# Branch projections of a hybrid encoder: loads handed out further ahead, four operand slots in an idle tile

## Chip, cores and metric

One NeuronCore of one Trainium2 chip runs the whole kernel. The metric is device time in microseconds (us) of one launch, the median of several runs. Everything is float32 at the interface.

## The reference, cut to what matters

One encoder layer over 1024 tokens (and 16 learned ones) of width 1024: a combined input projection, a gated DeltaNet branch A, a short-convolution branch B, a gated merge of the two, an output projection, and a SwiGLU. The change touches the place where the two branches are projected, merged and projected again:

```python
o = o * lax.rsqrt(jnp.mean(o * o, axis=-1, keepdims=True) + RMS_EPS) * norm_w
o = o * jax.nn.silu(z)                               # 8 heads of 128: (L, 1024)
y_a = o_dn @ w_branch_dn[l]
y_b = (sc_b * depthwise_conv_centred(sc_c * sc_x, sc_conv_w[l])) @ w_branch_sc[l]
merged = jax.nn.sigmoid(gate_a) * y_a + jax.nn.sigmoid(gate_b) * y_b
h_res = h_res + merged @ w_out[l]
```

## The kernel before, in words

**Splitting.** A float32 matrix product is done as three fast products: each operand is split into a high part (a cast on ScalarE, ACT: `hi`, here the ring `parts_h`) and a low part (VectorE, DVE, subtracts: `al`), and TensorE (PE) adds hi x hi, lo x hi and hi x lo (lines 1854 to 1856 in `products`, in varying order of the operands).

**Strassen-like quads.** Each of the two 1024 x 1024 x 1024 branch projections is done in seven products of half-size blocks (`QUADS`; S and T are sums of blocks, most of them prepared in DRAM). Each product of a quad has four 128-row tiles k of depth; two of them, a *k-pair*, make one **turn** q of the loop at the end of the stage. So a branch has 14 turns: 0 to 13 are branch B (z = 0), 14 to 27 are branch A (z = 1). A turn is 24 matmuls of 128 x 512. Turn pairs alternate between two groups of four PSUM banks, but turns 12, 13 and then 14, 15 use the same group.

**One turn.** `parts(q + 2)` casts and subtracts the operands of the turn after next (two tiles of 128 x 1024 each, so an `al` pair on DVE); `load(q + 4)` issues the DMAs of a later turn; `products(q)` is PE's work; `taken(q)`, after odd turns, copies or adds the four banks into running sums (`pv`, `us`) and, after four of the seven quads, multiplies them by gate tiles into `mA` and `mB`; `beside` lists the other work of the turn. The order of SPq (SyncE's DMA queue, on which all these DMAs are issued), DVE and ACT is the order in which this code is written (`manual_schedule`); only PE's order is chosen by a scheduler. In both kernels it puts the first four matmuls of turn 16 in front of turn 14, and six hi x hi and hi x lo products in front of the first product that needs `wl` in the output projection behind the stage (lines 1942 to 1944).

**Buffers.** `load` takes `rawtile` slots: four, in rotation. Branch B takes two of 512 KB per turn (four DMAs of 256 KB), branch A one. A slot is free when the `al` subtraction that reads it is done. `s4` tiles (four, in rotation) hold gate tiles and the z of a head. The large tiles `b0` to `b3` hold the first turns' operands (`b0`, `b1`), branch A's operand `og` (`b2`: heads 0 to 3, `b3`: heads 4 to 7), block sums of it (`b1`), and in the end the split `w_out` (`woh`, `wol`).

**Beside the turns.** `gated(h)` prepares head h of branch A: for h below 4 it only loads z (already multiplied); for h of 4 to 7 it loads o and z and multiplies them on DVE (line 1755) in the same place. `gate_tiles` loads four gate tiles; `block_sums` forms the sums of `og` (line 179); `out_load` and `out_split` load and split `w_out`, one of eight row tiles each; `merged(0)` splits the first rows of the merged result (`wh`, `wl`).

Of the kernel before, what the change touches and what calls it, by code (L numbers as in the profile page):

```python
# [8 lines left out]
F32 = mybir.dt.float32  # L9
# [3 lines left out]
ALU = mybir.AluOpType  # L13
# [3 lines left out]
P = 128  # L17
D = 1024
KT = 8
SEQ = 1024  # L20
# [8 lines left out]
ZH = 4  # L29
# [19 lines left out]
def encoder_layer(ctx: ExitStack, tc: tile.TileContext, x, meta, norm1_w, w_in, w_ba,  # L49
                  dn_conv_w, A_log, dt_bias, dn_norm_w, sc_conv_w, w_bdn, w_bsc,  # L50
                  w_out, norm2_w, w_gu, w_down, final_w, out):
    nc = tc.nc
    x, out = x[0], out[0]
# [11 lines left out]
    def uid(s):  # L65
        cnt["n"] += 1
        return f"{s}_{cnt['n']}"

    def s4(n=1024):
        return tp.tile([P, 1024], F32, tag="s4", name=uid("s4"), bufs=4)[:, :n]  # L70
# [29 lines left out]
    def split(hi, lo, src):  # L100
        nc.scalar.copy(hi, src)  # L101
        nc.vector.tensor_tensor(out=lo, in0=src, in1=hi.bitcast(F32), op=ALU.subtract)  # L102
# [3 lines left out]
    def rawtile(shape):  # L106
        raw_slots.append(raw_slots.pop(0))
        pool, tag = raw_slots[-1]
        return pool.tile(shape, F32, tag=tag, name=uid("raw"), bufs=1)
# [111 lines left out]
    z_d = [dr.tile([P, SEQ], F32, name=f"z_d{i}") for i in range(H)]  # L221
    o_d = [dr.tile([P, SEQ], F32, name=f"o_d{i}") for i in range(KT)]
# [4 lines left out]
    cols = keep.tile([P, 25], F32, name="cols")  # L227
# [854 lines left out]
    with tc.tile_pool(name="st", bufs=1) as st:  # L1082
# [7 lines left out]
        raw = st.tile([P, KT, 32], F32, name="wba_raw")  # L1090
# [371 lines left out]
    def big(tag, shape, dtype=F32R):  # L1462
        return tp.tile(shape, dtype, tag=tag, name=uid(tag))
# [239 lines left out]
        steps[k]()  # L1703
    border0.close()
    QUADS = (("A11", "B11"), ("A12", "B21"), ("S2", "T2"), ("S1", "T1"), ("S3", "T3"), ("S4", "B22"), ("A22", "T4"))
    loads = {}

    def load(q):

        z, n, kk = q // 14, q % 14 // 2, q % 2  # L1710
        a, b = QUADS[n]
        w, w_sums = ((w_bsc, ss_d), (w_bdn, sd_d))[z]
        plain = {"A11": (0, lo), "A12": (4, lo), "A22": (4, hi), "B11": (0, hi), "B21": (4, hi), "B22": (4, lo)}
        summed = {"S2": (0, lo), "S3": (0, hi), "S4": (1, lo), "S1": (1, hi), "T3": (0, lo), "T1": (0, hi), "T2": (1, lo), "T4": (1, hi)}
        loads[q] = []
        for x in (a, b)[:2 - z]:
            raw = rawtile([P, 2, 512])
            loads[q].append(raw)
            for i in range(2):
                k = 2 * kk + i  # L1720
                if x in plain:
                    r, c = plain[x]
                    src = w[(r + k) * P:(r + k + 1) * P, c] if x[0] == "A" else p_d[r + k][:, c]
                else:
                    r, c = summed[x]
                    src = (w_sums if x[0] == "S" else ts_d)[k][:, r, c]
                nc.sync.dma_start(raw[:, i], src)
# [11 lines left out]
        for i in range(2):  # L1739
            nc.sync.dma_start(ts_d[k][:, i], r[i])  # L1740

    og = []

    def gated(h):

        if not og:
            og.extend(big(f"b{2 + i}", [P, 4, SEQ], F32) for i in range(2))
        ot = og[h // 4][:, h % 4]
        if h < ZH:
            nc.sync.dma_start(ot, z_d[h])  # L1750
            return
        nc.sync.dma_start(ot, o_d[h])
        sz = s4(SEQ)
        nc.sync.dma_start(sz, z_d[h])
        nc.vector.scalar_tensor_tensor(out=ot, in0=ot, scalar=cols[:, 24:25], in1=sz, op0=ALU.mult, op1=ALU.mult)

    for n, j in enumerate(range(GH + 2, KT - 1), 2):
        d = pair_steps(n, j)[0]
        for i, k in enumerate(PAIR.split()):
            d[k]()  # L1760
            if i in (4, 16):
                state_sums(2 * n - 4 + i // 16)
    load(0)
    o1 = last_pair(KT - 1 - GH, KT - 1)

# [58 lines left out]
    woh, wol, raw_out = [], [], []  # L1824

    def out_load(j):
        raw_out.append(rawtile([P, D]))
        nc.sync.dma_start(raw_out[j], w_out[j * P:j * P + P, :])

    def out_split(j):  # L1830
        if j % 4 == 0:
            for w, tags in ((woh, ("b0", "b1")), (wol, ("b2", "b3"))):
                t = big(tags[j // 4], [P, 4, D])
                w.extend(t[:, k] for k in range(4))
        split(woh[j], wol[j], raw_out[j])
# [3 lines left out]
    def parts(q):  # L1839

        z, n, kk = q // 14, q % 14 // 2, q % 2
        operands[q] = *part(loads[q][0]), *part(loads[q][1] if z == 0 else o_blocks[QUADS[n][1]][:, 2 * kk:2 * kk + 2])

    def products(q):

        z, n, kk = q // 14, q % 14 // 2, q % 2
        bank = (bank_x, bank_y)[n % 2]
        fresh = n in (0, 1, 3)
        ah, al, bh, bl = operands[q]
        for t in range(4):  # L1850
            c = slice(t * P, t * P + P)
            for k in range(2):
                begin, end = kk + k == 0, kk + k == 2
                mm(bank[t], ah[:, k, c], bh[:, k], start=begin and fresh, stop=False, skip_group_check=not fresh)
                mm(bank[t], ah[:, k, c], bl[:, k], start=False, stop=False, skip_group_check=not fresh)
                mm(bank[t], al[:, k, c], bh[:, k], start=False, stop=end, skip_group_check=not fresh)

    def taken(q):

        z, n, kk = q // 14, q % 14 // 2, q % 2  # L1860
        bank = (bank_x, bank_y)[n % 2]
        if not kk:
            return
        if not pv:
            w = big("w2", [P, 2, 512], F32)
            pv.extend([w[:, 0], w[:, 1], *(tp.tile([P, 512], F32, tag="t2", name=uid("t2"), bufs=2) for _ in range(2))])
        if n == 2 and not us:
            w = [wp.tile([P, 2, 512], F32, tag=g, name=uid("us"), bufs=2) for g in ("wh", "wl")]
            us.extend(w[t // 2][:, t % 2] for t in range(4))
        for t, y in enumerate(bank):  # L1870
            if n in (0, 3):
                nc.scalar.copy(pv[t], y)
            elif n == 2:
                nc.scalar.copy(us[t], y)
            elif n in (1, 4):
                add(pv[t], y, pv[t])
            elif n == 5:
                add(us[t], y, us[t])
        if n not in where:
            return  # L1880
        r, c = where[n]
        for t in range(4):
            y, g, m_ = (us if n == 5 else bank if n == 6 else pv)[t], gates[z, n][t], mg[r // 4][:, t, c]
            nc.vector.scalar_tensor_tensor(out=g if z else m_, in0=g, scalar=1.0, in1=y, op0=ALU.add, op1=ALU.mult)
        if z:
            for t in range(4):
                m_ = mg[r // 4][:, t, c]
                add(m_, m_, gates[z, n][t])

    def merged(t):  # L1890
        mh, ml = wtiles([P, KT, P])
        for i in range(2):
            split(mh[:, 4 * i:4 * i + 4], ml[:, 4 * i:4 * i + 4], mg[i][:, :, t * P:(t + 1) * P])
        xr = s4(D)
        nc.sync.dma_start(xr, x[t * P:(t + 1) * P])
        return mh, ml, xr

    beside = {0: [(gated, 4)], 1: [(gate_tiles, 0, 1)], 2: [(gated, 5)], 3: [(gated, 6)], 4: [(gated, 0)], 5: [(gated, 7)],
              6: [(gate_tiles, 0, 4), (gated, 1)], 7: [(gated, 2)], 8: [(gated, 3), (gate_tiles, 0, 5)],
              9: [(block_sums, 0)], 10: [(block_sums, 1)], 11: [(gate_tiles, 0, 6)], 12: [(block_sums, 2)],  # L1900
              15: [(gate_tiles, 1, 1)], 16: [(block_sums, 3)], 18: [(out_load, 0)], 19: [(out_load, 1)],
              20: [(gate_tiles, 1, 4), (out_split, 0), (out_load, 2)], 21: [(out_split, 1), (out_load, 3)],
              22: [(gate_tiles, 1, 5), (out_split, 2), (out_load, 4)], 23: [(out_split, 3), (out_load, 5)],
              24: [(gate_tiles, 1, 6), (out_load, 6)], 25: [(out_split, 4), (out_split, 5), (out_load, 7)],
              26: [(out_split, 6), (out_split, 7)]}
    load(1)
    parts(0)
    parts(1)
# [4 lines left out]
    for q in range(28):  # L1913
        if q + 2 < 28:
            parts(q + 2)
        if q + 4 < 28:
            load(q + 4)
        products(q)
        if q == 27:
            first_rows = merged(0)  # L1920
        taken(q)
        for f, *a in beside.get(q, ()):
            f(*a)
# [56 lines left out]
    def part1(w, p1, sg):  # L1980

        rg, ru, A_ = w
        bank = pss()
        product(bank, A_["A11"], "B11")
        nc.scalar.copy(p1, bank)
        po = psz()
        product(po, A_["A12"], "B21")
        add(sg, po, p1)
        nc.scalar.activation(sg, sg, AF.Silu)
        return rg, ru, A_, p1, sg, bank  # L1990
# [191 lines left out]
    for j in range(2, NF):  # L2182
# [6 lines left out]
        else:  # L2189
            rg, ru, A_, p1, sg, b1 = part1(stationary1(j), sm[:, (j + 1) % 2], sm[:, 2 + (j + 1) % 2])  # L2190
# [4 lines left out]
        if j >= HK:  # L2195
            k = j - HK
# [166 lines left out]
```

## Time and profile before

| | us |
|---|---|
| median of 3 runs | 1981.32 (1979.26 to 1981.97) |
| the profiled execution, its own time | 1978.7 |
| its span, first to last instruction | 1977.0 |
| the changed stage, first to last matmul start | 1062.35 to 1240.81 |
| PE clock granted, mean of the span | 0.994 |

In the profile a line names an engine, a line of the code, an operation, what is written and read, and its shape; in a timeline the first two numbers are start and duration in us, and a bracket gives the idle time of that engine before the row and what ended it. SPq rows are DMA issues, not transfers. Rows of a line that stand together are merged (x2).

### The profile page before, as it was taken

Reading aid. Unit: us, or ns where it says so; the run is one execution under the profiler, and the core shown is the slowest. Engines: PE = TensorE matmul, PEld = TensorE weight load, DVE = VectorE, ACT = ScalarE, POOL = GpSimd, SP = SyncE. Lnnn points to the kernel's source line nnn. Section 1 sums busy time; section 2 is a strip of 40 time slices with the busy share of each in tenths; the row PEclk is TensorE's granted clock in tenths of the full one; section 3 lists DMA queues with packets and bytes.
Section 4 is the critical chain, followed back from the end, with each engine's and each line's share of the span. In section 5 each row is a group of like instructions: output and inputs, shape, how many; then the busy total and the mean of one; then the engine's idle time right before and its main releaser. Section 6 shows DMA issues by size and latency. Waiting matters only on the chain. (4 is left out here: it accounts for less than half of the span.)

```text
span 1977.0 us, 32151 instructions
## 1 busy us (share of the span) xinstructions
PE 1942.7 (98%) x11896; PEld 1706.0 (86%) x11896; DVE 1477.2 (75%) x3121; ACT 875.2 (44%) x2016; POOL 109.2 (6%) x410
## 2 busy tenths in 40 slices
PE   9999999999999999999999789999999999999998
PEld 8999999999999999888888668788888888888887
DVE  7888688888888888868963488669676766746575
ACT  6462364646464645343434345235332333324344
POOL 2011101010101010100000000000000000000000
PEclk9999999999999999999999899999999999999999
DMA  4122122212121223376367656223366654487654
GB/s 145 63 84 81 56 85 60 83 52 85 51 87 50 86 59 98 108 264 241 111 246 252 225 203 208 96 86 116 119 224 249 243 185 163 170 277 244 192 177 164
DMA packets 141987, 286.15 MB, mean 145 GB/s; under 512 B 46909, under 2 KB 48374, under 8 KB 138374
## 3 DMA queue, kind: packets, MB, share of 16 engines
q1 hardware_dynamic: 141237, 283.05, 42.7%
q8 instruction: 93, 1.52, 0.3%
q10 hardware_dynamic: 592, 1.05, 0.1%
q14 instruction: 65, 0.52, 0.1%
HBM read 203.22 MB, written 80.83 MB: 144 GB/s over the span
## 5 line engine op out<-in xcount | busy, mean ns | idle before, releaser
L343 PE MATMUL pm<-hTh,wl 128*128 128x320 f32 (+4 forms) x1248 | 426.9, 347 | 0.1
L343 PE MATMUL pm<-hTh,wh 128*128 128x320 f32 (+4 forms) x1248 | 426.5, 347 | 0.4 <-ACT hTh L1150 0.2
L343 PE MATMUL pm<-al,wh 128*128 128x320 f32 (+4 forms) x1248 | 424.2, 345 | 0.0
L343 PEld LDWEIGHTS pm<-hTh,wh 128*128 128x128 f32 x1248 | 233.9, 189 | 10.9 <-ACT hTh L1150 0.9
L343 PEld LDWEIGHTS pm<-al,wh 128*128 128x128 f32 x1248 | 233.8, 188 | 10.8
L343 PEld LDWEIGHTS pm<-hTh,wl 128*128 128x128 f32 x1248 | 233.9, 188 | 9.9 <-POOL wl L1165 0.3
L102 DVE TENSOR_TENSOR al<-raw,ring_h 128x1024 fp32r<-128x1024 f32 x73 | 88.8, 1223 | 65.0 <-ACT ring_h L101 64.2
L101 ACT CAST ring_h<-raw 128x1024 fp32r<-128x1024 f32 x73 | 76.7, 1053 | 106.8 <-PE pd L2272 38.6
L365 DVE SCALAR_TENSOR_TENSOR kq<-ra,wc,kq 128x520 f32<-128x520 f32 x128 | 96.7, 755 | 3.5 <-ACT kq L395 2.0
L1003 DVE TENSOR_TENSOR wl<-raw,wh 128x512 fp32r<-128x512 f32 x112 | 75.1, 686 | 29.8 <-ACT wh L1006 29.6
L898 ACT ACTIVATE w<-pd,small 128x128 f32<-128x128 f32 x128 | 40.0, 363 | 124.3 <-PE pd L891 123.8
L503 DVE TENSOR_TENSOR tm<-fP,fN 128x135 f32<-128x135 f32 (+23 forms) x248 | 72.2, 291 | 4.8
L507 DVE TENSOR_TENSOR fP<-fP,tm 128x135 f32<-128x135 f32 (+23 forms) x248 | 71.9, 290 | 5.0
L1006 ACT CAST wh<-raw 128x512 fp32r<-128x512 f32 x112 | 66.0, 624 | 3.8 <-issue 3.6
L101 ACT CAST parts_h<-raw 128x1024 fp32r<-128x1024 f32 x36 | 37.7, 1051 | 64.6 <-DMA raw<-ss_d 34.5
L2210 ACT ACTIVATE b<-b 128x512 f32<-128x512 f32 x20 | 12.6, 632 | 105.0 <-DVE b L1470 105.0
L102 DVE TENSOR_TENSOR al<-raw,parts_h 128x1024 fp32r<-128x1024 f32 x36 | 42.9, 1220 | 19.1 <-ACT parts_h L101 19.1
L863 ACT ACTIVATE jk<-NP 128x128 f32<-128x128 f32 x64 | 19.9, 311 | 78.9 <-DVE NP L859 77.9
L1470 DVE TENSOR_TENSOR b<-pd,b 128x512 f32<-128x512 f32 x21 | 14.5, 690 | 51.6 <-PE pd L1504 51.5
L1504 PE MATMUL pd<-b_hl,wh 128*128 128x512 f32 x168 | 51.9, 390 | 0.0
L365 DVE SCALAR_TENSOR_TENSOR vT<-ra,wc,vT 128x520 f32<-128x520 f32 x64 | 48.3, 755 | 1.4 <-ACT vT L395 0.7
L699 POOL TENSOR_TENSOR tm<-mP,mN 1x15 f32<-1x15 f32 (+7 forms) x120 | 36.9, 308 | 211.3 <-DMA mN<-ndm 202.9
(698 smaller groups left out, 4861.0 us busy)
## 6 DMA issues: line engine op xcount, KB each, us to landing
raw<-in_w_in_dram SPq DMA_DIRECT2D x72, 512.0 KB
raw<-in_w_gate_up_dram SPq DMA_DIRECT2D x44, 512.0 KB
sums<-in_w_down_dram SPq DMA_DIRECT2D x22, 512.0 KB
t_d<-sums SPq DMA_DIRECT2D x11, 1024.0 KB
raw<-s_d SPq DMA_DIRECT2D x44, 256.0 KB
raw<-t_d SPq DMA_DIRECT2D x44, 256.0 KB
act_d<-b SPq DMA_DIRECT2D x43, 256.0 KB
raw<-act_d SPq DMA_DIRECT2D x33, 256.0 KB
```

Source lines behind the costliest of these rows:

```text
L101: nc.scalar.copy(hi, src)
L102: nc.vector.tensor_tensor(out=lo, in0=src, in1=hi.bitcast(F32), op=ALU.subtract)
L343: mm(po[:, :n], ww[:, k], f(k)[:, t0:t0 + n], start=i == 0, stop=i == 3 * KT - 1)
L365: nc.vector.scalar_tensor_tensor(out=acc, in0=raw[:, h0 + t:h0 + t + hn], scalar=wc[:, t, col:col + 1], in1=acc, op0=ALU.mult, op1=ALU.add)
L503: nc.vector.tensor_tensor(out=tv, in0=fP[:, 0:r, j:j + 1].broadcast_to([P, r, n]), in1=fN[:, j:j + 1, j + 1:32].broadcast_to([P, r, n]), o ...
L507: nc.vector.tensor_tensor(out=fP[:, 0:r, j + 1:32], in0=fP[:, 0:r, j + 1:32], in1=tv, op=ALU.subtract)
L699: nc.gpsimd.tensor_tensor(out=tv, in0=mP[:, 0:j + 1, j:j + 1].broadcast_to([1, j + 1, n]), in1=mN[:, j:j + 1, j + 1:META].broadcast_to([1, ...
L863: nc.scalar.activation(jk, oacc[c], AF.Square, accum_out=sso[:, c:c + 1])
L898: nc.scalar.activation(w[d], b2[:, 2 + d], AF.Copy, scale=ce[:, c, d:d + 1])
L1003: nc.vector.tensor_tensor(out=u[1][1][:, k], in0=u[2][:, k], in1=u[1][0][:, k].bitcast(F32), op=ALU.subtract)
L1006: nc.scalar.copy(u[1][0][:, k], u[2][:, k])
L1504: mm(po, x[:, k], at(y, k), start=i == 0 and not add_to, stop=i == 11, skip_group_check=add_to)
```

## The change

`load` is given out two turns further ahead: load(q + 6) in turn q instead of load(q + 4), apart from the first turns (4, 5, 6, then 7 and 8, then 9 and 10). The operands of turns 8, 9, 12 and 13 go into four quarters of `b0` instead of the four raw slots. `gated` is cut in two: `head_load` issues the DMAs, `gated` does the multiplication one or more turns later. The first four `w_out` tiles are loaded into the same quarters of `b0`, from turn 16 on; their splits move from turns 20 to 23 to turns 22 to 24; the split `w_out` lies in `b2`, `b0` (high) and `b1`, `b3` (low). The first two block sums move from turns 9 and 10 to turns 10 and 11.

```diff
+    def quarter(i):
+        if not corner_b0:
+            corner_b0.append(big("b0", [P, 4, D], F32))
+        return corner_b0[0][:, i]
...
-        for x in (a, b)[:2 - z]:
-            raw = rawtile([P, 2, 512])
+        for j, x in enumerate((a, b)[:2 - z]):
+            if q in (8, 9, 12, 13):
+                raw = quarter(2 * (q % 2) + j).rearrange("p (k c) -> p k c", k=2)
+            else:
+                raw = rawtile([P, 2, 512])
...
-        nc.sync.dma_start(ot, o_d[h])
-        sz = s4(SEQ)
-        nc.sync.dma_start(sz, z_d[h])
-        nc.vector.scalar_tensor_tensor(out=ot, in0=ot, scalar=cols[:, 24:25], in1=sz, op0=ALU.mult, op1=ALU.mult)
+        nc.sync.dma_start(og[1][:, h - 4], o_d[h])
+        head_z[h] = s4(SEQ)
+        nc.sync.dma_start(head_z[h], z_d[h])
+
+    def gated(h):
+        ot = og[1][:, h - 4]
+        nc.vector.scalar_tensor_tensor(out=ot, in0=ot, scalar=cols[:, 24:25], in1=head_z[h], op0=ALU.mult, op1=ALU.mult)
...
-        raw_out.append(rawtile([P, D]))
+        raw_out.append(quarter(j) if j < 4 else rawtile([P, D]))
...
-            for w, tags in ((woh, ("b0", "b1")), (wol, ("b2", "b3"))):
+            for w, tags in ((woh, ("b2", "b0")), (wol, ("b1", "b3"))):
...
-    beside = {0: [(gated, 4)], 1: [(gate_tiles, 0, 1)], 2: [(gated, 5)], 3: [(gated, 6)], 4: [(gated, 0)], 5: [(gated, 7)],
-              6: [(gate_tiles, 0, 4), (gated, 1)], 7: [(gated, 2)], 8: [(gated, 3), (gate_tiles, 0, 5)],
...
+    beside = {0: [(head_load, 4)], 1: [(gate_tiles, 0, 1)], 2: [(gated, 4), (head_load, 5)], 3: [(head_load, 6)],
+              4: [(gated, 5), (head_load, 0)], 5: [(gated, 6), (head_load, 7)], 6: [(gate_tiles, 0, 4), (head_load, 1)],
+              7: [(gated, 7), (head_load, 2)], 8: [(head_load, 3), (gate_tiles, 0, 5)],
...
-        if q + 4 < 28:
-            load(q + 4)
+        for i in {0: (4,), 1: (5,), 2: (6,), 3: (7, 8), 4: (9, 10)}.get(q, (q + 6,)):
+            if i < 28:
+                load(i)
```

What that does to the engines' rows. First DVE, from the end of turn 3's products with the gates (`mA`) on, before. `al<-raw` are the operands' low parts in the order of the turns, two a turn, from turn 6 on; L1755 multiplies a head:

```order
L1884 SCALAR_TENSOR_TENSOR mA_13151<-s_2196_13281,t_2194_13275 128x512
L1755 SCALAR_TENSOR_TENSOR b_2185_13230<-b_2185_13230,cols,s_2202_13367 128x1024
L102 TENSOR_TENSOR al_13238<-raw_13290,parts_h 128x1024
L102 TENSOR_TENSOR al_13238<-raw_13293,parts_h 128x1024
L102 TENSOR_TENSOR al_13236<-raw_13328,parts_h 128x1024
L102 TENSOR_TENSOR al_13236<-raw_13331,parts_h 128x1024
L1755 SCALAR_TENSOR_TENSOR b_2185_13230<-b_2185_13230,cols,s_2209_13446 128x1024
L102 TENSOR_TENSOR al_13236<-raw_13374,parts_h 128x1024
L102 TENSOR_TENSOR al_13236<-raw_13377,parts_h 128x1024
```

And the same place of DVE now (L1896 is L1884 of before, L1767 is L1755; `b_2202` is the quartered `b0`):

```order
L1896 SCALAR_TENSOR_TENSOR mA_13151<-s_2196_13280,t_2194_13274 128x512
L102 TENSOR_TENSOR al_13237<-raw_13289,parts_h 128x1024
L102 TENSOR_TENSOR al_13237<-raw_13292,parts_h 128x1024
L1767 SCALAR_TENSOR_TENSOR b_2185_13230<-b_2185_13230,cols,s_2199_13321 128x1024
L102 TENSOR_TENSOR al_13235<-raw_13327,parts_h 128x1024
L102 TENSOR_TENSOR al_13235<-raw_13330,parts_h 128x1024
L1767 SCALAR_TENSOR_TENSOR b_2185_13230<-b_2185_13230,cols,s_2203_13371 128x1024
L102 TENSOR_TENSOR al_13235<-b_2202_13333,parts_h 128x1024 x2
L102 TENSOR_TENSOR al_13236<-b_2202_13333,parts_h 128x1024 x2
L1767 SCALAR_TENSOR_TENSOR b_2185_13230<-b_2185_13230,cols,s_2210_13455 128x1024
```

Before, head 6 stood ahead of turn 6's pair and head 7 ahead of turn 8's; now pair 6, head 5, pair 7, head 6, pairs 8 and 9, head 7. (The first such row, head 4's, stood ahead of pair 3 and stands behind pair 4.)

On SPq, the DMAs from head 5's z to head 6's, before (o_d and z_d are the head's loads, ss_d and ts_d hold the S and T operands):

```order
L1754 DMA s_2199_13321<-z_d_104 128x1024
L1727 DMA raw_13328<-ss_d_129 128x512
L1727 DMA raw_13328<-ss_d_130 128x512
L1727 DMA raw_13331<-ts_d_125 128x512
L1727 DMA raw_13331<-ts_d_126 128x512
L1752 DMA b_2185_13230<-o_d_113 128x1024
L1754 DMA s_2202_13367<-z_d_105 128x1024
```

And now, on SPq:

```order
L1762 DMA s_2199_13321<-z_d_104 128x1024
L1736 DMA raw_13327<-ss_d_129 128x512
L1736 DMA raw_13327<-ss_d_130 128x512
L1736 DMA raw_13330<-ts_d_125 128x512
L1736 DMA raw_13330<-ts_d_126 128x512
L1736 DMA b_2202_13333<-ss_d_127 128x512
L1736 DMA b_2202_13333<-ss_d_128 128x512
L1736 DMA b_2202_13333<-ts_d_123 128x512
L1736 DMA b_2202_13333<-ts_d_124 128x512
L1760 DMA b_2185_13230<-o_d_113 128x1024
L1762 DMA s_2203_13371<-z_d_105 128x1024
```

Behind load 7 there is now load 8, into `b0`, ahead of head 6.

At the stage's end, DVE before, from the split of a `w_out` tile in turn 24 to the next sums (`al` of turns 26 and 27):

```order
L102 TENSOR_TENSOR b_2243_14013<-raw_14055,b_2242_14012 128x1024
L102 TENSOR_TENSOR al_13238<-raw_14061,parts_h 128x1024
L102 TENSOR_TENSOR al_13238<-b_2185_13230,parts_h 128x1024
L102 TENSOR_TENSOR al_13236<-raw_14102,parts_h 128x1024
L102 TENSOR_TENSOR al_13236<-b_2185_13230,parts_h 128x1024
L1470 TENSOR_TENSOR us_13439<-pe_13157,us_13439 128x512
```

And the same place of DVE now:

```order
L102 TENSOR_TENSOR b_2239_14081<-b_2202_13333,b_2238_14080 128x1024
L102 TENSOR_TENSOR al_13237<-raw_13978,parts_h 128x1024
L102 TENSOR_TENSOR al_13237<-b_2185_13230,parts_h 128x1024
L102 TENSOR_TENSOR b_2239_14081<-b_2202_13333,b_2238_14080 128x1024
L102 TENSOR_TENSOR al_13235<-raw_14015,parts_h 128x1024
L102 TENSOR_TENSOR al_13235<-b_2185_13230,parts_h 128x1024
L1470 TENSOR_TENSOR us_13447<-pe_13157,us_13447 128x512
```

One more `w_out` split stands between the `al` pairs; behind these sums four splits follow in both kernels, and then `wl` of `merged(0)`. From there on the rows of all engines are the same in both, apart from which of `b0` to `b3` the output projection reads.

More of the change, by code (lines that the diff above doesn't have):

```diff
@@ L1705, in encoder_layer @@
     QUADS = (("A11", "B11"), ("A12", "B21"), ("S2", "T2"), ("S1", "T1"), ("S3", "T3"), ("S4", "B22"), ("A22", "T4"))
-    loads = {}
+    loads, corner_b0 = {}, []
+    def quarter(i):
+        if not corner_b0:
+            corner_b0.append(big("b0", [P, 4, D], F32))
+        return corner_b0[0][:, i]
     def load(q):
@@ L1740, in state_sums, with head_load @@
             nc.sync.dma_start(ts_d[k][:, i], r[i])
-    og = []
-    def gated(h):
+    og, head_z = [], {}
+    def head_load(h):
         if not og:
             og.extend(big(f"b{2 + i}", [P, 4, SEQ], F32) for i in range(2))
-        ot = og[h // 4][:, h % 4]
         if h < ZH:
-            nc.sync.dma_start(ot, z_d[h])
+            nc.sync.dma_start(og[0][:, h], z_d[h])
             return
-        nc.sync.dma_start(ot, o_d[h])
-        sz = s4(SEQ)
-        nc.sync.dma_start(sz, z_d[h])
-        nc.vector.scalar_tensor_tensor(out=ot, in0=ot, scalar=cols[:, 24:25], in1=sz, op0=ALU.mult, op1=ALU.mult)
+        nc.sync.dma_start(og[1][:, h - 4], o_d[h])
[4 more added lines that the diff above has]
+        nc.vector.scalar_tensor_tensor(out=ot, in0=ot, scalar=cols[:, 24:25], in1=head_z[h], op0=ALU.mult, op1=ALU.mult)
     for n, j in enumerate(range(GH + 2, KT - 1), 2):
@@ L1896, in merged @@
         return mh, ml, xr
-    beside = {0: [(gated, 4)], 1: [(gate_tiles, 0, 1)], 2: [(gated, 5)], 3: [(gated, 6)], 4: [(gated, 0)], 5: [(gated, 7)],
-              6: [(gate_tiles, 0, 4), (gated, 1)], 7: [(gated, 2)], 8: [(gated, 3), (gate_tiles, 0, 5)],
[L1900 to L1905, printed above, removed]
+    beside = {0: [(head_load, 4)], 1: [(gate_tiles, 0, 1)], 2: [(gated, 4), (head_load, 5)], 3: [(head_load, 6)],
+              4: [(gated, 5), (head_load, 0)], 5: [(gated, 6), (head_load, 7)], 6: [(gate_tiles, 0, 4), (head_load, 1)],
+              7: [(gated, 7), (head_load, 2)], 8: [(head_load, 3), (gate_tiles, 0, 5)],
+              10: [(block_sums, 0)], 11: [(gate_tiles, 0, 6), (block_sums, 1)], 12: [(block_sums, 2)],
+              15: [(gate_tiles, 1, 1)], 16: [(block_sums, 3), (out_load, 0)], 17: [(out_load, 1)], 18: [(out_load, 2)],
+              19: [(out_load, 3)], 20: [(gate_tiles, 1, 4)], 22: [(gate_tiles, 1, 5), (out_split, 0), (out_split, 1), (out_load, 4)],
+              23: [(out_split, 2), (out_load, 5)], 24: [(out_split, 3), (gate_tiles, 1, 6), (out_load, 6)],
+              25: [(out_split, 4), (out_split, 5), (out_load, 7)], 26: [(out_split, 6), (out_split, 7)]}
     load(1)
```

## The prediction

> **What bounds the kernel now.** I read the page first, then the waits of TensorE (PE), then stretches around those waits, and last the timelines of PE, VectorE (DVE), ScalarE (ACT) and of the DMA queue (SPq).
>
> ```profile
> span 1977.0 us, 32151 instructions
> PE 1942.7 (98%) x11896; PEld 1706.0 (86%) x11896; DVE 1477.2 (75%) x3121; ACT 875.2 (44%) x2016; POOL 109.2 (6%) x410
> ```
>
> PE is the bound, so only what it loses counts. Waits of PE, longest in total first (total, times, longest):
>
> ```profile
> PE pd L1855 <- DVE al L102: 7.4, 3, 3.5
> PE pe L1855 <- DVE al L102: 5.5, 1, 5.5
> PE pd L1854 <- DVE mB L1884: 3.6, 1, 3.6
> PE pe L1942 <- ACT wh L101: 3.1, 1, 3.1
> PE pe L1854 <- ACT parts_h L101: 1.6, 1, 1.6
> ```
>
> L1854 and L1855 are the changed stage's matmuls; L1942 is the first product behind it. Next, PE's rows in time (start, duration, idle before in brackets):
>
> ```profile
> 1062.35 0.39 PE L1854 MATMUL pd<-b 128*128 128x512 f32 x1
> ...
> 1065.07 0.39 PE L1854 MATMUL pe<-b 128*128 128x512 f32 x1
> ...
> 1093.10 0.79 PE L1855 MATMUL pd<-al,parts_h 128*128 128x512 f32 x1 [2.48 <-DVE al L102]
> 1093.69 0.63 PE L1856 MATMUL pd<-parts_h,al 128*128 128x512 f32 x1
> ...
> 1096.38 0.40 PE L1855 MATMUL pd<-al,parts_h 128*128 128x512 f32 x1
> ...
> 1147.27 0.50 PE L1855 MATMUL pd<-al,parts_h 128*128 128x512 f32 x1 [1.39 <-DVE al L102]
> ...
> 1159.12 0.50 PE L1854 MATMUL pe<-parts_h 128*128 128x512 f32 x1 [1.58 <-ACT parts_h L101]
> 1163.89 0.80 PE L1854 MATMUL pd<-parts_h 128*128 128x512 f32 x1 [3.56 <-DVE mB L1884]
> ...
> 1240.81 0.39 PE L1856 MATMUL pm<-parts_h,al 128*128 128x512 f32 x1
> 1244.32 0.50 PE L1942 MATMUL pe<-b,wh 128*128 128x512 f32 x1 [3.12 <-ACT wh L101]
> ...
> 1245.94 0.39 PE L1944 MATMUL pe<-b,wl 128*128 128x512 f32 x1
> ```
>
> The first two rows stand 12 matmuls and 2.72 us apart: 0.2267 us each, 5.44 us for a turn of 24. The 28 turns (672 matmuls) need 152.34 us; call N(q) = 1062.35 + 5.44q the start of turn q without any loss, so N(28) = 1214.69. The last matmul ended at 1240.81 + 0.23 = 1241.04. **The stage loses 26.35 us**: the first, second, third and fifth of those waits, 18.1 us, and slow matmuls after some of them (0.63 us long at 1093.69 instead of 0.39). This is all that the change can win there.
>
> Why PE waited stands in DVE and SPq:
>
> ```profile
> 1072.00 1.28 DVE L1755 SCALAR_TENSOR_TENSOR b<-b,cols,s 128x1024 f32<-128x1024 f32 x1 [8.76 <-DMA s<-z_d]
> ...
> 1089.49 1.28 DVE L1755 SCALAR_TENSOR_TENSOR b<-b,cols,s 128x1024 f32<-128x1024 f32 x1 [11.65 <-DMA s<-z_d]
> 1090.69 2.35 DVE L102 TENSOR_TENSOR al<-raw,parts_h 128x1024 fp32r<-128x1024 f32 x2
> ...
> 1137.86 1.28 DVE L1470 TENSOR_TENSOR w<-pd,w 128x512 f32<-128x512 f32 x2
> ...
> 1142.66 2.29 DVE L179 TENSOR_TENSOR b<-b,b 128x2048 f32<-128x2048 f32 x1
> ...
> 1163.15 1.28 DVE L1884 SCALAR_TENSOR_TENSOR mB<-s,pd 128x512 f32<-128x512 f32 x2
> ```
> ```profile
> SPq L1727 <- DVE al L102: 77.3, 19, 9.7
> ...
> 1074.45 0.80 SPq L1727 DMA_DIRECT2D raw<-ss_d  x2
> ```
> ```profile
> 1064.04 1.03 ACT L101 CAST parts_h<-raw 128x1024 fp32r<-128x1024 f32 x1
> ...
> 1073.43 0.59 ACT L1872 COPY t<-pm 128x512 f32<-128x512 f32 x1 [0.77 <-PE pm L1856]
> 1073.91 2.00 ACT L101 CAST parts_h<-raw 128x1024 fp32r<-128x1024 f32 x2
> 1078.61 1.05 ACT L101 CAST parts_h<-raw 128x1024 fp32r<-128x1024 f32 x1 [2.70 <-DMA raw<-ss_d]
> ```
>
> It is a ring of waits: DVE stands before L1755 until that head's z has landed; the `al` subtractions behind it stand too; the raw buffers that they would free keep SPq standing (77.3 us in the stage); and so the next loads, the next z among them, start late. Transfers that are not held up are fast (columns: length, busy of PE, PEld, DVE, ACT, POOL, PE clock, DMA share, GB/s):
>
> ```profile
> 1062.35:1241.20 178.85, 160.86 (x673) 130.31 (x671) 118.43 (x130) 72.29 (x84) 0.00 (x0) 0.94 0.63 213
> ...
> 1095.00:1100.00 5.00, 5.00 (x21) 3.92 (x19) 2.84 (x5) 1.54 (x2) 0.00 (x0) 0.90 0.91 292
> 1127.00:1142.00 15.00, 15.00 (x68) 12.41 (x67) 8.14 (x11) 5.26 (x5) 0.00 (x0) 1.00 1.04 386
> ```
>
> **The change, part by part.** It removes and adds no arithmetic and no bytes; rows move.
>
> *Head loads and gating apart.* A head's gated multiply now stands one to three turns behind its load, and behind `al` rows that are due first. The first `al` rows no longer wait for 1072.00: their casts are done by 1065.1 (the row at 1064.04), so load 5 goes out near 1066 instead of 1074.45. Load 6 must wait for the slots of load 4, whose casts stand behind the bank copies on ACT: cast from 1073.91, 1.05 us, one `al` of 1.22: **1076.2**. From there the queue has 9.96 MB up to head 7's z (loads 6 to 11 with heads 5 to 7 at 1.05 MB each, z of head 0 at 0.52) and 15.2 MB up to head 3's z. A lone load took 1074.45 to 1078.61, 4.16 us for 0.52 MB, thus 2.8 us fixed beside 1.36 at 386 GB/s. So head 7's z lands at 1076.2 + 2.8 + 25.8 = 1104.8, head 3's at 1118.4.
>
> *Does PE still wait in turns 4 to 13?* By DVE's new order: a bank can be read 0.2 us after its turn (1073.43 against N(2) = 1073.23), the sums and products of turn 9 took 4.80 us for eight rows (1137.86 to 1142.66), 0.6 each, so those of turn 3 end near N(4) + 0.2 + 5 x 0.6 = 1087.3; the `al` pair of load 6 (2.35 us, row at 1090.69), one gating (1.2, 1089.49 to 1090.69), pair 7, a gating, pairs 8 and 9 end near 1101; they are due at N(6) = 1095, N(7) = 1100.4, N(9) = 1111.3, each with over 6 us to spare. After head 7's gating the pairs 10 and 11 end near 1112, held by ACT, whose casts stand behind turn 7's copies (due 1116.8). No wait: the 26.35 us go.
>
> *The four slots in b0.* Loads 8, 9, 12, 13 take them and need no raw slot, so the queue need not stand at them: load 8 needs only PE's turn 2 done (1078.7). Their price is nil, since the tile's readers before are done by then. Moving `w_out`'s first four loads there frees raw slots later; the swap of tiles changes only which of `b0` to `b3` the projection reads.
>
> *What is late next: DVE's own chain at turn 14.* Turn 14 writes the bank that turn 13's mB rows read. From the first sum of turn 9 (1137.86) to mB of turn 13 (1163.15) DVE had no gap: 25.29 us, the same rows after the change (the block sums stand one `al` pair later). The last sum of turn 9 cannot start before N(10) + 0.2 = 1116.96; four sums of 0.6 then make the chain's start 1115.16, mB 1140.45, and PE follows 0.74 later (1163.15 to 1163.89): 1141.19. PE is there at N(14) + 0.91 = 1139.43, having done four matmuls of turn 16. **A wait of 1.76 us stays.** It holds if head 7's z is there by 1109.4 (1115.16 less one gating and four `al`) and head 3's by 1122.2 (1115.16 plus turn 9's 4.80, 1137.86 to 1142.66, and one `al` pair): 4 us of slack, which needs 352 GB/s; at 292 head 3's z lands at 1131.1, and 8.9 us are lost again.
>
> *Clock.* After the 2.48 us wait nine matmuls began from 1093.10 to 1096.38, 3.28 us for eight steps of 0.2267: 1.47 us lost. After 1.39 us idle the first is 0.50 long, not 0.79, and 1.76 is nearer to that: 0, with 1.5 as the other end. The Trainium skill, "TensorE: Matmul & The Clock Gate", Part 1, says that the clock halves after at least one idle window of about 3.4 us. By that rule 1.76 us costs nothing, and 2.48 us should not have either: there the trace disagrees, so the upper end stays.
>
> *The tail.* Rows of DVE:
>
> ```profile
> 1219.48 0.69 DVE L1470 TENSOR_TENSOR t<-pm,t 128x512 f32<-128x512 f32 x1 [0.62 <-PE pm L1856]
> ...
> 1224.90 1.22 DVE L102 TENSOR_TENSOR b<-raw,b 128x1024 fp32r<-128x1024 f32 x1
> 1226.04 1.22 DVE L102 TENSOR_TENSOR al<-raw,parts_h 128x1024 fp32r<-128x1024 f32 x1
> ...
> 1230.58 0.68 DVE L1470 TENSOR_TENSOR us<-pe,us 128x512 f32<-128x512 f32 x1
> ...
> 1237.79 3.49 DVE L102 TENSOR_TENSOR b<-raw,b 128x1024 fp32r<-128x1024 f32 x3
> ...
> 1243.78 1.23 DVE L102 TENSOR_TENSOR b<-raw,b 128x1024 fp32r<-128x1024 f32 x1 [2.50 <-ACT b L101]
> 1244.92 0.69 DVE L102 TENSOR_TENSOR wl<-mA,wh 128x512 fp32r<-128x512 f32 x1
> ```
>
> Turn 24 began at 1241.04 - 21.76 = 1219.28; the sums behind it end 5.6 later, `wl` starts 25.64 later. Now: 5.6, then six rows of 1.14 (two `w_out` splits, four `al`), 7.2 (1230.58 to 1237.79), four splits 4.55: `wl` at 24.2, **1.4 us earlier**, provided that the last `w_out` load lands under the 7.2. Bounds: 3.5 us won (no wait left: 1245.94 less 1241.04 less the six matmuls that go first) and 1.1 lost (the 2.50 us before the last split come back).
>
> **Sum.** 1978.7 (this execution's own time; its span is 1977.0) - 26.35 + 1.76 + 0 - 1.4 = 1952.7. The median of the runs is 1981.3, 2.6 above this execution: 1955.3. All slack at turn 14 rests on one transfer rate; I put 0.7 us on it: **1956**.
>
> **Rivals.** *The queue comes late to turn 14.* For it: 15.2 MB in the 43 us from 1079 to 1122.2 is nearly all that the DMA has shown, and each hold of SPq eats the 4 us. Against it: 386 GB/s over 15 us with the same sizes. At 292 GB/s: 1955.3 + 8.9 = 1964; with holds as well up to 1970.
>
> *Slower: the new order makes the heads' last z the bound.* All of DVE's chain now follows head 3's z. Were the rate the stage's mean of 213 GB/s, it would land at 1079 + 71.4 = 1150.4, mB 18.2 us later (25.29 less turn 9's sums and one pair) at 1168.6, 5.4 behind 1163.15 less the tail's 1.4: 1985. It decides below 226 GB/s. Against it: 213 is a mean over 63% of the DMA's time. The Trainium skill, "DMA: Bandwidth & Descriptors", Anatomy of one DMA, gives each DMA some 2 us fixed plus bytes at 436 GB/s: 256 KB one after another, an estimate of 100 GB/s, would make this case far worse. The 386 GB/s row shows them overlapped, so only the lone first load pays it.
>
> *Nothing changes.* If loads still left only when the `al` two turns before had run, and these still stood behind a gating. Loads 5 to 7 do use the same raw slots. But the new order puts the gating behind the pairs 3 and 4, whose data was there. It would give 1981.
>
> **Chances.** First case 0.72 (1952 to 1961: tail and clock bounds, up to 5 us of lateness); late queue 0.21 (1961 to 1972); nothing 0.03; slower 0.04. A change within 0.2% (4 us) cannot be told from none. Faster 0.93, same 0.03, slower 0.04. The range 1952 to 1968 leaves out the last two cases, the late end of the second, and little below.
>
> **What would show it.** Right: no wait of the L1855 matmuls for `al` between turns 5 and 12; SPq's wait for `al` well under 77 us; one wait of about 1.8 us before turn 14 for mB; the stage 154 us long; a wait of about 2 us behind it. Wrong: DVE standing at the gating of head 7 or at the first block sum for a z; a DMA rate under 350 GB/s in the 45 us from load 6 on; a cast that waits for a `b0` load.

## The result and the profile after

| | before | after |
|---|---|---|
| median of the runs, us | 1981.62 (1979.26 to 1981.97, 4 runs) | **1952.99** (1952.75 to 1953.23, 4 runs) |
| ratio after / before, 95% | | 0.9858 [0.9841, 0.9875] |
| the profiled execution, own time, us | 1978.7 | 1953.22 |
| its span, us | 1977.0 | 1951.5 |

The kernel is 1.4% faster: 28.6 us between the medians, 25.5 us between the two profiled executions. The forecast was 1956.0 (1952 to 1968). The page after, head and busy times:

```profile
span 1951.5 us, 32154 instructions
PE 1934.0 (99%) x11896; PEld 1701.0 (87%) x11896; DVE 1477.7 (76%) x3121; ACT 875.0 (45%) x2016; POOL 108.7 (6%) x410
```

The work is the same (11896 matmuls); the span lost PE's idle time and some slow matmuls. PE's waits after, those of the stage and right behind it (total, times, longest):

```profile
PE pe L1957 <- DVE wl L102: 1.6, 1, 1.6
PE pd L1866 <- DVE mB L1896: 1.6, 1, 1.6
```

All the waits for `al` and `parts_h` (7.4, 5.5, 1.6 us before) are gone; L1867, which is L1855 of before, isn't in the list. The two that are left, in PE's timeline, with the stage's first and last matmul:

```profile
1062.58 0.39 PE L1866 MATMUL pd<-b 128*128 128x512 f32 x1
...
1141.42 0.50 PE L1866 MATMUL pd<-parts_h 128*128 128x512 f32 x1 [1.61 <-DVE mB L1896]
...
1216.85 0.39 PE L1955 MATMUL pe<-b,wh 128*128 128x512 f32 x1
...
1220.02 0.50 PE L1957 MATMUL pe<-b,wl 128*128 128x512 f32 x1 [1.65 <-DVE wl L102]
```

The stage starts at 1062.58 (0.23 later than in the execution of before) and ends at 1216.85: 154.27 us instead of 178.69. DVE, with the gated multiplies now at L1767:

```profile
1107.13 1.28 DVE L1767 SCALAR_TENSOR_TENSOR b<-b,cols,s 128x1024 f32<-128x1024 f32 x1 [5.51 <-DMA s<-z_d]
1108.33 4.62 DVE L102 TENSOR_TENSOR al<-raw,parts_h 128x1024 fp32r<-128x1024 f32 x4
...
1117.18 0.69 DVE L1470 TENSOR_TENSOR t<-pm,t 128x512 f32<-128x512 f32 x1 [0.67 <-PE pm L1868]
...
1122.46 2.29 DVE L179 TENSOR_TENSOR b<-b,b 128x2048 f32<-128x2048 f32 x1
...
1140.68 1.28 DVE L1896 SCALAR_TENSOR_TENSOR mB<-s,pd 128x512 f32<-128x512 f32 x2
...
1219.26 0.70 DVE L102 TENSOR_TENSOR wl<-mA,wh 128x512 fp32r<-128x512 f32 x1
```

DVE still stands before a head's multiply (5.51 us before head 7's). Behind it stand the `al` pairs of turns 10 and 11, but they are done at 1112.95, 4.0 us before turn 10 begins (1062.58 + 10 x 5.44 = 1116.98). From the last sum of turn 9 (1117.18) to mB (1140.68) it has no gap. SPq's wait in the stage (of the `load` line, total, times, longest) and its issue of load 6:

```profile
SPq L1736 <- DVE al L102: 44.9, 13, 10.0
...
1076.48 0.80 SPq L1736 DMA_DIRECT2D raw<-ss_d  x2
```

And the stretch from load 6 to head 3's z (columns: length, busy of PE, PEld, DVE, ACT, POOL, PE clock, DMA share, GB/s):

```profile
1079.00:1118.00 39.00, 39.00 (x174) 32.30 (x173) 27.51 (x30) 19.54 (x24) 0.00 (x0) 1.00 1.03 377
```

The DMA engines are full there: 377 GB/s over 39 us, where the same stage of before had a mean of 213.

### The profile page after: what moved, and what is told of

It is laid out like the page before. It is cut to its first block, busy times and chain, and to the rows that moved or that the text cites. A ratio compares the mean times of both kernels' runs of the same rounds, so it can differ in the third digit from the quotient of the medians.

```text
span 1951.5 us, 32154 instructions
## 1 busy us (share of the span) xinstructions
PE 1934.0 (99%) x11896; PEld 1701.0 (87%) x11896; DVE 1477.7 (76%) x3121; ACT 875.0 (45%) x2016; POOL 108.7 (6%) x410
## 4 chain that ended last, share of the span: by engine, by line
PE 90%; DVE 4%; DMA 3%; issue 1%; ACT 1%; SPq 0%; POOL 0%; DVEq 0%; ACTq 0%; POOLq 0%
PE pm L343 32%; PE pd L1504 14%; PE pe L1504 7%; PE pm L1504 5%; PE pd L912 1%; PE pd L891 1%; PE pd L876 1%; PE pd L873 1%; PE pe L610 1%; PE pe L2284 1%; PE pe L2285 1%; PE pe L2283 1%; PE pd L908 1%; PE pd L2284 1%; PE pd L2285 1%
## 5 line engine op out<-in xcount | busy, mean ns | idle before, releaser
L102 DVE TENSOR_TENSOR al<-raw,parts_h 128x1024 fp32r<-128x1024 f32 x28 | 33.7, 1223 | 24.4 <-ACT parts_h L101 24.4
L1504 PE MATMUL pd<-b_hl,wh 128*128 128x512 f32 x168 | 51.9, 390 | 0.0
L553 ACT ACTIVATE PQ<-PQ,negG 128x128 f32<-128x128 f32 x128 | 43.1, 396 | 8.1 <-DVE PQ L548 7.7
```

Of the source, the lines that this page charges most:

```text
L553: nc.scalar.activation(PQ[:, c, d], PQ[:, c, d], AF.Exp, bias=negG2[:, c, hd:hd + 1])
L1504: mm(po, x[:, k], at(y, k), start=i == 0 and not add_to, stop=i == 11, skip_group_check=add_to)
```

## The experiments

Theory A: only the cut of `gated` counts. It takes DVE's stand for a z out of the way of the `al` rows, and the ring (DVE, raw slots, SPq, z) opens. Rivals: the slots in `b0` and the longer lead do it; or the gain hangs on the DMA rate with no slack.

### e1: the cut alone

Before, with `head_load` and `gated` at after's places, and the first two block sums one turn later, as in after; loads still q + 4, raw slots and `w_out` as before.

```diff
-    beside = {0: [(gated, 4)], ... 2: [(gated, 5)], 3: [(gated, 6)], 4: [(gated, 0)], 5: [(gated, 7)],
+    beside = {0: [(head_load, 4)], ... 2: [(gated, 4), (head_load, 5)], 3: [(head_load, 6)],
+              4: [(gated, 5), (head_load, 0)], 5: [(gated, 6), (head_load, 7)], ... 7: [(gated, 7), (head_load, 2)],
...
-              9: [(block_sums, 0)], 10: [(block_sums, 1)], 11: [(gate_tiles, 0, 6)], 12: [(block_sums, 2)],
+              10: [(block_sums, 0)], 11: [(gate_tiles, 0, 6), (block_sums, 1)], 12: [(block_sums, 2)],
```

> The kernel before, with one part of the change alone: heads are loaded and multiplied in two places, as in the changed kernel (and the first two block sums one turn later); loads stay two turns ahead in the raw slots, w_out as before. Theory A (the gain is the gating's place: DVE no longer stands at a z ahead of operand rows that are due): the raw slots suffice; by the rows of the changed kernel load 8 leaves when pair 6 is done (1089.9), load 9 near 1093.4, and all pairs are still in time. About 1954.5 us, the changed kernel's 1953.0 and 1.4 for the tail; SPq's wait for al in the stage stays near 60 us without costing PE anything. Theory B (the four more slots and the longer lead are what feeds the turns): most waits of PE before turn 12 return, 1965 us or more.

Measured: 1955.22 us (1953.06 to 1955.86), ratio 0.9869 [0.9854, 0.9884]; the profiled execution 1953.06, as after's 1953.22. PE's waits in and right behind the stage, and SPq's:

```profile
PE pe L1946 <- ACT wh L101: 2.8, 1, 2.8
PE pd L1857 <- DVE mB L1887: 1.6, 1, 1.6
...
SPq L1727 <- DVE al L102: 52.3, 23, 9.0
```

The same 1.6 us before turn 14, no wait for `al`. So **the cut alone brings nearly the whole gain**; the slots and the lead aren't needed for it. The later block sums alone don't bring it: e2 has them too.

### e2: slots and lead without the cut

After, with a head's load and multiplication in one place again.

```diff
-    beside = {0: [(head_load, 4)], ... 2: [(gated, 4), (head_load, 5)], 3: [(head_load, 6)], ...
+    beside = {0: [(gated, 4)], ... 2: [(gated, 5)], 3: [(gated, 6)], 4: [(gated, 0)], 5: [(gated, 7)], ...
```

> The changed kernel with a head loaded and multiplied in one place again, at the turns of before (heads 4, 5, 6, 0, 7 at turns 0, 2, 3, 4, 5); the four slots in b0, the longer lead and the w_out loads stay. Theory A: DVE stands again before each L1755 row; since load 8 or loads 9 and 10 now stand ahead of the z of heads 6 and 7 in the queue, these waits are as long as before or longer: 1975 to 1990 us. Theory B: at least half of the 28.6 us gain stays: 1967 us or less.

Measured: 1976.23 us (1975.11 to 1977.60, 9 runs), ratio 0.9975 [0.9965, 0.9985]. The first of its gated multiplies on DVE (line 1764 here), then PE's longest waits and SPq's:

```profile
1072.89 1.28 DVE L1764 SCALAR_TENSOR_TENSOR b<-b,cols,s 128x1024 f32<-128x1024 f32 x1 [9.37 <-DMA s<-z_d]
```
```profile
PE pd L1864 <- DVE al L102: 4.1, 1, 4.1
PE pd L1863 <- ACT parts_h L101: 3.8, 1, 3.8
...
SPq L1736 <- DVE al L102: 73.6, 17, 10.0
```

DVE stands 9.37 us before head 4's multiply, SPq 73.6 us: the ring is still closed, though four loads need no raw slot and all go out two turns further ahead. The first rival falls.

### e3 and e4: 1 and 4 MB more on the queue

After, with 4 (e3) and with 16 (e4) loads of 256 KB into `b1`, unread, half ahead of head 0's z and half ahead of head 7's.

```diff
+    def extra(n):
+        ...
+            nc.sync.dma_start(spare[0][:, k], p_d[k][:, lo])
-              4: [(gated, 5), (head_load, 0)], 5: [(gated, 6), (head_load, 7)], ...
+              4: [(gated, 5), (extra, 2), (head_load, 0)], 5: [(gated, 6), (extra, 2), (head_load, 7)], ...   # e4: 8 and 8
```

> The changed kernel with four more loads of 256 KB (1.05 MB that nobody reads) into the idle tile b1, two ahead of head 0's z and two ahead of head 7's in the queue. If the rate of the queue sets when head 7's z lands (1107.1 in the changed kernel's trace, with DVE's chain to turn 14 needing it by 1109.4): 2.7 us later at 386 GB/s, 1109.8, so 0 to 1 us slower: 1953 to 1954 us. Rival (the queue is not the limit, the slots are): z lands as before, 1953.0 us and the wait at the gating stays 5.5 us.

> The same with sixteen loads (4.2 MB), eight ahead of each. At 386 GB/s head 7's z lands 10.9 us later, at 1118.0, 8.6 us after DVE's chain needs it: PE loses about 8.6 us at turns 10 to 14, and up to 2 us more at the half clock: 1961 to 1964 us. If the rate falls to 213 GB/s when more is asked: 20 us later, 1970 us or more. If the queue is not the limit: 1953 to 1955 us.

Measured: e3 1955.38 us (1953.05 to 1957.38), e4 1965.69 (1963.21 to 1966.25), both 1.4 to 1.7 us above the ranges expected. Head 7's multiply and the first block sum on DVE in e3, then PE's turn 14:

```profile
1109.62 1.28 DVE L1778 SCALAR_TENSOR_TENSOR b<-b,cols,s 128x1024 f32<-128x1024 f32 x1 [7.96 <-DMA s<-z_d]
...
1123.13 2.29 DVE L179 TENSOR_TENSOR b<-b,b 128x2048 f32<-128x2048 f32 x1 [0.54 <-DMA b<-z_d]
...
1142.08 0.50 PE L1877 MATMUL pd<-parts_h 128*128 128x512 f32 x1 [2.23 <-DVE mB L1907]
1143.38 0.63 PE L1879 MATMUL pd<-parts_h,al 128*128 128x512 f32 x1
...
1146.76 0.39 PE L1878 MATMUL pe<-al,parts_h 128*128 128x512 f32 x1
```

And the same in e4, with the wait for `al` that comes before:

```profile
1117.73 1.28 DVE L1778 SCALAR_TENSOR_TENSOR b<-b,cols,s 128x1024 f32<-128x1024 f32 x1 [16.28 <-DMA s<-z_d]
...
1121.35 0.50 PE L1878 MATMUL pe<-al,parts_h 128*128 128x512 f32 x1 [3.46 <-DVE al L102]
...
1150.56 0.80 PE L1877 MATMUL pd<-parts_h 128*128 128x512 f32 x1 [5.55 <-DVE mB L1907]
```

1 MB moves head 7's z by 2.49 us (1107.13 to 1109.62), but PE's wait at turn 14 grows only by 0.62, about what the first block sum waits for head 3's z (0.54): the rest is slack. The wait was not all that e3 paid: eight matmuls from 1143.38 to 1146.76 begin some 0.42 us apart instead of 0.23, and the stage takes 156.45 us (1062.62 to 1219.07), 2.18 more than in after, 0.6 of them in the wait and 1.6 in these slow matmuls. 4 MB move it by 10.6 us and the slack is used up; the profiled execution is 13 us longer, 7.4 of them in PE's waits (3.46 + 5.55 - 1.61), the rest mostly (4.4 us, in the stage) in slow matmuls behind these two waits. That is the "late queue" of the prediction's first rival, produced on purpose: it is real, and after has some 2 us of slack before it, not the 4 that the prediction gave it.

### e5: after once more, beside the next three

> The changed kernel once more, on the same chip as the three that follow, so that differences of 1 to 3 us can be read. Theory A and its rival alike: 1953.0 us, PE waiting 1.6 us before turn 14 for mB and 1.65 us behind the stage for wl.

Measured: 1953.61 us (1951.91 to 1957.82), before on this chip 1979.19 (1977.60 to 1984.41), ratio 0.9868 [0.9849, 0.9888]; waits of 1.6 us both, as expected.

### e6: `w_out` as before

After, with `w_out`'s loads, splits and tiles as before.

```diff
-        raw_out.append(quarter(j) if j < 4 else rawtile([P, D]))
+        raw_out.append(rawtile([P, D]))
-              ... 16: [(block_sums, 3), (out_load, 0)], 17: [(out_load, 1)], 18: [(out_load, 2)], ...
+              ... 18: [(out_load, 0)], 19: [(out_load, 1)], 20: [..., (out_split, 0), (out_load, 2)], 21: [(out_split, 1), ...
```

> After, with w_out's eight loads and splits back at the places and in the tiles of before. Theory A (the tail's term of 1.4 us is these six to eight rows): the wait behind the stage goes from 1.65 back to about 2.8 to 3.1 us, and the time from 1953.0 to 1954.2 to 1954.4. Rival (the tail is set by the sums behind turn 27, wherever w_out is split): no change, 1953.0. A wait of DVE for ACT before the last split would speak for the first.

Measured: 1960.02 us (1959.14 to 1961.61): 6.4 us slower than e5, neither theory's number. ACT's casts of `w_out` (b) and behind them those that PE needs, then what PE does, and then SPq's issue of that `w_out` tile with the row ahead of it:

```profile
1208.16 1.05 ACT L101 CAST b<-raw 128x1024 fp32r<-128x1024 f32 x1 [7.44 <-DMA raw<-in_w_out_dram]
1209.11 1.04 ACT L101 CAST parts_h<-raw 128x1024 fp32r<-128x1024 f32 x1
```
```profile
1211.15 1.22 PE L1866 MATMUL pd<-parts_h 128*128 128x512 f32 x2 [3.46 <-ACT parts_h L101]
```
```profile
1201.23 0.81 SPq L1736 DMA_DIRECT2D raw<-in_w_branch_dn_dram  x2
1202.09 0.43 SPq L1840 DMA_DIRECT2D raw<-in_w_out_dram  x1
```

The stage takes 160.38 us (1063.43 to 1223.81) against 154.23 in e5: some 4 of these 6.15 us are PE's wait of 3.46 and one of 0.46 for `al`, the rest slow matmuls. It is the mistake that the change takes out of the stage's first half, made in its second half: ACT stands 7.44 us for a `w_out` load, and casts that PE needs stand behind it. The load left late (1202.09), because operand loads two turns further ahead stand in front of it on SPq, and these wait for raw slots (theory B, tried in e9). So the longer lead needs after's way of loading `w_out`. Which part of it (the quarters of `b0`, the earlier turns, or both) this run doesn't tell: it takes back both, and the swap of tiles.

### e7: the third block sum two turns later

After with one edit (the text below calls it the third head's; it is the third of `og`'s block sums):

```diff
-              ... 12: [(block_sums, 2)],
+              ... 14: [(block_sums, 2)],
```

> After, with the block sums of the third head (one DVE row of some 2.3 us and its ACT rows) at turn 14 instead of turn 12. Theory A (the wait of 1.6 us before turn 14 is the length of DVE's own chain from the sums of turn 9 to mB of turn 13, with nothing in it waiting): the chain is 2.3 us shorter, the wait goes, and the time is 1951.4. Rival (the wait is PE's own distance from turn 13, or a transfer): the wait stays at 1.6 us, 1953.0. A third way: what was moved lies ahead of the next due rows, and a wait of 1 to 2 us comes in a later turn, 1952 to 1954.

Measured: 1951.35 us (1950.18 to 1952.96). DVE's mB, and the only wait of PE left in or right behind the stage:

```profile
1138.17 1.27 DVE L1896 SCALAR_TENSOR_TENSOR mB<-s,pd 128x512 f32<-128x512 f32 x2
...
PE pe L1957 <- DVE wl L102: 1.6, 1, 1.6
```

mB starts 2.5 us earlier than in after (2.2 against the stage's start, 0.31 earlier here), and the wait of 1.6 us before turn 14 is gone: it was the length of DVE's chain. The profile carries this; the runs of e5 and e7 overlap (from 1951.91 and up to 1952.96).

### e8: both waits

e7, and the merge of turn 27 ahead of the last two splits:

```diff
-              25: [(out_split, 4), (out_split, 5), (out_load, 7)], 26: [(out_split, 6), (out_split, 7)]}
+              25: [(out_split, 4), (out_split, 5), (out_load, 7)]}
...
             first_rows = merged(0)
+            out_split(6)
+            out_split(7)
```

> The one before, and the merge of the last sums placed ahead of the last two splits of w_out, so that DVE's chain to wl is some 2.3 us shorter. Theory A (both waits that are left are lengths of DVE's chain): wl is there when PE comes, the wait of 1.65 us behind the stage goes too, and the time is 1949.8. Rival (wl waits for ACT's cast of wh or for pm's copies, not for DVE's queue): the wait shrinks by under 0.5 us; or PE then waits for the two last splits instead: 1951 to 1953.

Measured: 1950.61 us (1950.15 to 1952.30). PE at the stage's end, and far behind it:

```profile
1215.19 0.39 PE L1957 MATMUL pe<-b,wh 128*128 128x512 f32 x1
...
1480.64 3.02 PE L1504 MATMUL pd<-b,w 128*128 128x512 f32 x12 [0.87 <-DVE b L1470]
```

The stage lasts 152.32 us (1062.87 to 1215.19), 672 matmuls of 0.2267, and the wait for `wl` is gone. But the time lies between the 1949.8 of theory A and its rival's 1951: the medians of e7 and e8 differ by 0.7 us, not 1.6, and so do the spans of the profiled executions, counted from the stage's start (886.2 and 885.5). The rest comes back as 0.87 us here (0.36 in e7) and 0.40 us at 1745 (none in e7): 0.9 us of new waits for DVE.

### e9: e6 with the shorter lead in the second half

```diff
-        for i in {0: (4,), 1: (5,), 2: (6,), 3: (7, 8), 4: (9, 10)}.get(q, (q + 6,)):
+        for i in {0: (4,), ..., 5: (11,), 6: (12,), 7: (13,), 8: (), 9: ()}.get(q, (q + 4,)):
```

> The kernel of e6 (w_out at the places and in the tiles of before), with the loads of the second half four turns ahead of their readers instead of six: those up to k-pair 13 go out as in after, none in turns 8 and 9, then k-pair q + 4 in turn q. Theory B (e6 lost its 6.4 us because w_out's loads stood in SPq's queue behind operand loads of two turns more, which had to wait for raw slots, so the w_out casts came late and stood on ACT ahead of the casts PE needed): the waits for parts_h and al in turns 20 to 27 go, DVE or ACT wait under 3 us for a w_out load, the wait behind the stage is 2.8 us as in e1, and the time is 1953.0 to 1955.5. Rival (the swap of the tiles b0 to b3, or w_out in raw slots as such, costs it): the wait of 3.5 us for parts_h stays, 1958 to 1960.

Measured: 1957.70 us (1956.90 to 1958.73). The 3.46 us for `parts_h` is gone, as theory B says (the fourth `w_out` load leaves at 1186.97, not at 1202.09): the stage lost 1.61 us at turn 14 and nothing else. The time misses its range by 2.2 us, behind the stage: PE's first row there, and the stretch from 1220.5 to 1230 in e9 and then in e1 (columns as above, PE clock third from the end):

```profile
1220.02 0.56 PE L1956 MATMUL pe<-b,wh 128*128 128x512 f32 x1 [3.27 <-ACT wh L101]
```
```profile
1220.50:1230.00 9.50, 9.50 (x37) 7.66 (x36) 7.89 (x14) 1.02 (x2) 0.00 (x0) 0.83 0.16 55
```
```profile
1220.50:1230.00 9.50, 9.50 (x43) 7.65 (x42) 8.00 (x14) 0.93 (x2) 0.00 (x0) 1.00 0.17 57
```

After 3.27 us of waiting the granted clock is 0.83 and six matmuls fewer begin in 9.5 us, worth 1.4 us; e1, after 2.85 us at the same place, keeps 1.00. Counted from the stage's start, e9's profiled execution is 4.3 us longer than e1's (892.9 and 888.6): those 1.4, 0.4 of longer wait, and 2.0 in two later waits for DVE (1.2 us at L1504, 0.8 at L2285) that e1's doesn't have; 0.5 I can't place. So e6's loss in the stage is settled; why e9's later waits are there is not.

### e10: the cut and the two moves, nothing else

e1's kernel with the edits of e7 and e8.

> The kernel of e1 (loads and gating apart, loads four turns ahead, no b0 slots, w_out as before) with the two moves of e8: block sums of the third head at turn 14, the merge of the last sums ahead of the last two splits of w_out. Theory A (both waits left over are lengths of DVE's chain, and the b0 slots and the longer lead have no part in the gain): both waits go, 1949.8 to 1951, as e8. Rival (in e1 the wait behind the stage is for wh from ACT, held by a late w_out load, and stays): 1951.5 to 1953.

Measured: **1949.59 us** (1948.75 to 1951.11, 5 runs), before on this chip 1981.92 (9 runs), ratio 0.9838 [0.9824, 0.9851]. PE at turn 14, and at the stage's end:

```profile
1141.10 0.39 PE L1859 MATMUL pd<-parts_h,al 128*128 128x512 f32 x1
...
1215.22 0.39 PE L1947 MATMUL pe<-b,wh 128*128 128x512 f32 x1
```

From 1062.90 to 1215.22, 152.32 us: the stage has no loss left. The rival (wh held by a late `w_out` load) falls: with two splits out of its way, wh is there in time; in the wait list of PE no line of the stage or of the projection behind it is left. This kernel is faster than before, and its median is 3.4 to 4.0 us below after's two, with fewer edits than the change has. Against before on its own chip, though, its interval overlaps those of after (0.9858 [0.9841, 0.9875]), of after in e5 and of e8 (0.9852 [0.9835, 0.9868]): that it beats after rests on the waits that are gone from its profile, and whether it beats e8 the intervals don't tell.

## Why the prediction was right, step by step

- **Bound, ring of waits, 26.35 us.** Right, and shown: the cut alone opens the ring (e1), all the rest without it does not (e2). SPq's wait fell from 77.3 to 44.9 us.
- **Load 5, load 6, head 7's z, head 3's z.** Load 5 left at 1065.28 (near 1066 forecast), load 6 at 1076.48 (1076.2 forecast, and the stage began 0.23 later). Head 7's z came at 1107.1, not 1104.8: 2.1 us later after that shift. The rate from 1079 on was 377 GB/s where I took 386 from a stretch of 15 us; on 9.96 MB that is 0.6 us. Of the other 1.5 us, 0.9 are in load 6 itself (from its issue at 1076.48 to the cast that it releases, ACT's at 1081.50, 5.02 us, where 4.16 was taken); the rest I can't place. Head 7's z lies inside the bound of 1109.4 forecast for it, so it cost nothing; e3 and e4 show where it would. Head 3's z was there before 1122.46, where the first block sum starts without a wait. One of the prediction's signs of being wrong did appear, DVE's stand at the gating of head 7 (5.51 us), with the rest of the forecast intact: the sign was badly chosen. By the forecast's own rows, pairs 8 and 9 end near 1101 and the z lands at 1104.8, so DVE had to stand there some 3.8 us. The other signs stayed away (no wait at the first block sum; 367 GB/s from 1076.5 to 1121.5; no cast waited for a `b0` load).
- **The rival "slower".** It falls on the measured rates, 386 and 377 GB/s, far from the 226 at which it would begin. The Trainium skill, "DMA: Bandwidth & Descriptors", Anatomy of one DMA, which the prediction weighs there, gives its fixed 2 us for transfers that GpSimd issues; those here are SyncE's.
- **Turn 14.** mB at 1140.68 and PE at 1141.42: forecast 1140.45 and 1141.19, and the 0.23 later start makes both exact. By the row PE is idle for 1.61 us; counted from start to start, as the forecast was, 1.77 are lost (the matmul before began at 1139.42), against 1.76. e7 shows that it is DVE's chain.
- **Clock.** Forecast 0: right, with luck in it. After 1.61 us the first matmul is 0.50 long and the next ones are at full speed: the stage lost 1.93 us (154.27 - 152.34), the 1.77 and 0.16 more. But the other end, 1.5, was near: with 0.6 us more of idle time e3 lost 1.6 us to slow matmuls. The Trainium skill, "TensorE: Matmul & The Clock Gate", Part 1, was weighed there, and this row agrees with it; e3's and e9's rows do not (2.23 and 3.27 us are under its window of about 3.4 us; matmuls slowed behind both, and in e9 the clock fell to 0.83).
- **The tail.** Turn 24 began at 1216.85 - 21.76 = 1195.09, and `wl` 24.17 us later: forecast 24.2. The term is a little under-sized: 1.4 us were forecast, but PE gets past its wait 1.73 us earlier against the stage's end (4.90 us before, 1220.02 - 1216.85 = 3.17 after), since before PE had six more matmuls to do after wh came.
- **"The four slots in b0: price nil."** No price in after, but the step is incomplete: with the longer lead, `w_out` loaded as before costs 6.4 us (e6); the prediction said of that part of the change only that it "frees raw slots later".
- **The sum and 1956.** 1952.7 for the profiled execution against 1953.22: off by 0.5, and of that 0.23 is the later start. What was wrong is the last step, median over profiled execution: the 2.6 us that before's median lay above its profiled run did not carry over (after: 1952.99 against 1953.22), and the 0.7 us put on the DMA rate wasn't lost. Those two terms, 3.3 us, make the error of 3.0 us (3.3 less the 0.5 above, plus the 0.2 by which after's median lies under its profiled run). The medians of one kernel on different chips differ by as much (before 1979.19 to 1981.92 here). A part of the spread is one wait of PE ahead of the stage, for a tile `xr`: 0.4 us in the profile of e5, 2.0 in that of e9. What sets the rest is open.

## What to carry to other kernels

On an engine whose order is written out, an instruction that waits for a transfer also holds everything behind it, and if that frees the buffers of the next transfers, the wait feeds itself: put the load where it was and the reader behind the work that is due, before buying more buffers or a longer lead. A longer lead is not free either: loads that must wait for a slot stand in front of others in the same queue (e6). When the big waits are gone, look at the chain of the engine that is late by 1 to 2 us and move what isn't due out of it (e7, e8, e10), but count on some of it coming back later.

## What the runs showed of the hardware that I had not expected

The clock does not go by the length of a wait alone: matmuls ran at about half their rate for some 3 to 4 us after waits of 2.23 us (e3, 1.6 us lost, from 1.3 us behind the wait on), 2.48 us (before, 1.47 us lost) and 3.27 us (e9, clock 0.83), and did not after 2.85 us (e1, clock 1.00) or 1.61 us (after), all with PE busy ahead of the wait. A wait of 2 to 3 us can thus cost half as much again or more, and a forecast has to hold both ends. What decides it these runs don't show. And one core's DMA engines kept 377 GB/s over 39 us, with transfers of 256 KB and 512 KB on one queue.
